# The output projection's second token tile: gates multiplied from SBUF, its operands in attention's buffers

## The chip, the cores and the metric

The kernel runs on one core of a Trainium2 chip. The metric is the device time of one execution in microseconds (us), from the device's own clock.

## What is computed

One transformer block on 1024 tokens of width 1024, all in float32:

```python
h = rmsnorm(x, g_mix_pre)
proj = h @ w_in
qa, ka, va, gate_a, beta_a, alpha_a, qb, kb, vb = split(proj)
out_a = gated_deltanet(...) * silu(gate_a)      # 4 heads x 128
out_b = dilated_attention(qb, kb, vb, rel_bias) # 8 heads x 64
mix = concatenate([out_a, out_b]) @ w_out       # the output projection
x = x + rmsnorm(mix, g_mix_post)
h = rmsnorm(x, g_ffn_pre)
x = x + rmsnorm((silu(h @ w_gate) * (h @ w_up)) @ w_down, g_ffn_post)
```

## The kernel before, in words

**How the program is made.** Every piece of work is a Python generator, a strand, that yields one instruction after another. A scheduler in the kernel file keeps a modelled clock for each engine, takes at each step the strand whose next instruction can start first (with priorities, and on TensorE with a margin of 850 ns for operands that would only just be there), and so fixes each engine's order of instructions when the program is built. On the chip each engine runs its list in that order, and an instruction that waits for a semaphore holds everything behind it on its engine. All large transfers are issued from SyncE (SP, "SPq" in the profile), one list in order.

**The order of the work.** The input projections (tiles `pj`), then the delta-rule chain and the attention beside the last projections, then the output projection, then the gated feed-forward layer (gate and up products and the down product, PSUM tiles `bank`). The feed-forward products are made by a seven-product scheme on 2 x 2 blocks.

**Matrix products in three parts.** Each float32 operand is split into a high part (a cast, `mh`, `woh`, `wbh`) and a low part (a subtraction, `ml`, `wol`, `wbl`); a product takes three matmuls, high x high, high x low, low x high (`mm3`).

**The output projection** (`out_proj`, line 1809) runs over eight token tiles t of 128 tokens. The mixer's 1024 channels come in two parts: part 0 is the delta rule's four heads, part 1 the attention's. A tile has two column halves b of 512, and for each half and part 4 channel blocks x 3 matmuls of 128 x 512 into the PSUM tile `pw`: 48 matmuls a tile. Tile 0 takes them in the order part 0 for both halves, then part 1 for both; the others take part 0 and part 1 of half 0, then of half 1. When a half is done ScalarE copies it out (`evacuate`, tile `y`).

**What feeds it** (`mix_load`, line 1738; `mix_loads` runs it for t = 0 to 7, part 0 then part 1, one strand, each load requested once the one before has issued its split). For each tile and part: load `mx` (256 KB) from the DRAM tensor `d_mix`; for part 1, multiply by `rp`, the softmax denominators spread over PSUM by four small matmuls; for part 0, multiply by the gates; then split into `mh` and `ml`. The gates lie in SBUF tiles `gst`. `gate_silu` (line 837) applies SiLU to them and stores all eight to DRAM (`d_gt`). Tile 0 multiplies straight from the four `gst` tiles that hold tokens 0 to 511 (`first`), one 128 x 128 multiply for each head; then `first_done` releases them. Every later tile waits until all gates are projected (`ev_gates`), and loads its gates back from `d_gt` into a tile `gt` (one 128 x 512 multiply).

**Buffers.** `mx` of tile 0 lies in a small pool `ax`, that of all others in two slots (`mxS`) which are also the last two gates' buffers (`rawS.slots[:2]`, line 1668); so such a load waits until those gates are stored. `mh` and `ml` of the others take slots `mixS`.

**Afterwards** (`residual`, line 1842): for each tile load `x3` (the block's input, two halves), square sum of `y` (`junk`), multiply by `gpost`, `n_m` and `n_r` (an inverse root: DVE, then GpSimd), add (`x`, two halves), second square sum, second `n_r`, scale (`y`), eight transposes on TensorE (two groups of four, `tp`), which ScalarE copies to `h2s` for tiles 0 to 3 and stores as `d_h2`.

**The feed-forward's start.** `ev_ax` fires when tile 0's matmuls are issued (line 1829). The build then closes the pool stack `s2`, which holds attention's pool `at` and `ax` (line 1899), and takes the feed-forward's pools in that memory; only then are its strands made, the weight loads (`wraw`) and splits (`wbh`, `wbl`) among them. The first four `wraw` loads come in that way amid the output projection; the matmuls that use them begin when all eight tiles are through.

Of the kernel before, what the change touches and what calls it, by code (L numbers as in the profile page):

```python
# [11 lines left out]
F32 = mybir.dt.float32  # L12
F32R = mybir.dt.float32r
BF16 = mybir.dt.bfloat16
AF = mybir.ActivationFunctionType
ALU = mybir.AluOpType
# [5 lines left out]
P = 128  # L22
# [24 lines left out]
SB = 4  # L47
XB = 3
# [11 lines left out]
def sub(ap, dims, off=0):  # L60
    return bass.AP(tensor=ap.tensor, offset=ap.offset + off, ap=[list(d) for d in dims])
# [480 lines left out]
def block_kernel(ctx: ExitStack, tc: tile.TileContext, a, out):  # L542
    nc = tc.nc
    w = Weaver(nc)
    T, V, A, G, SY = (Engine(w, e, k) for e, k in (
        (nc.tensor, "PE"), (nc.vector, "V"), (nc.scalar, "A"), (nc.gpsimd, "G"), (nc.sync, "S")))
    ctx.enter_context(tc.manual_schedule(engines={ENG.PE, ENG.DVE, ENG.Activation, ENG.Pool, ENG.SP}))

    def mm(out, lhsT, rhs, start=True, stop=True):
        return T.matmul(out, lhsT, rhs, start=start, stop=stop)  # L550

    def tr(out, in_):
        return T.transpose(out, in_, ident[:])

    def mm3(ps, lh, ll, rh, rl, first, last):
        return [mm(ps, lh, rh, first, False), mm(ps, lh, rl, False, False), mm(ps, ll, rh, False, last)]
# [9 lines left out]
    def split_sb(hi, lo, src):  # L566
        yield Either(A.copy(hi, src), V.tensor_copy(hi, src), bias=BIAS)
        yield Either(*[e.tensor_tensor(lo, src, hi.bitcast(F32), ALU.subtract) for e in (V, G)])

    def pool(stack, name, bufs, space=None, side=None):  # L570
        return Pool(w, stack, tc, name, bufs, space, side)
# [256 lines left out]
    gates, silued, silu, first = [], [], set(), {}  # L828
# [526 lines left out]
    at = pool(s2, "at", 2)  # L1355
# [310 lines left out]
    woS, mixS, mxS, x3S = (Slots(wp, "", 0) for _ in range(4))  # L1666
# [66 lines left out]


    axS = Slots(pool(s2, "ax", 1), "ax", 5)
    mixes = {}
    ev_mix = [[Event() for _ in range(2)] for _ in range(NT)]
    def mix_load(t, part):

        tl = slice(t * P, (t + 1) * P)  # L1740
        if part:
            for m in range(PAIRS):
                yield ev_att[m][t // 2]
        else:
            yield ev_o[t]
        if t:
            yield ev_gates
        x = yield (mxS if t else axS).get([P, 4, P], F32, name="mx")
        yield SY.dma_start(x[:], d_mix[4 * part:4 * part + 4, :, tl].rearrange("k p j -> p k j"))
        if part:  # L1750

            if t % 4 == 0:
                r = psums[:, t:t + 4, :]
                yield V.reciprocal(r, r)
                yield from split_sb(rtok[:, :, 0:AH], rtok[:, :, AH:2 * AH], r)
                tp = yield banks.get([P, P], F32, name="rt")
                yield tr(tp[:], rtok[:].rearrange("p t k -> p (t k)").bitcast(F32))
                for k in range(4):

                    x32 = rrow[32 * k:32 * k + 32, k, :]  # L1760
                    yield A.copy(sub(x32, [list(x32.ap[0]), [-1, 4], [-4, 32]], 127),
                                 tp[32 * k:32 * k + 32, :].rearrange("p (r j) -> p r j", r=4))
                banks.put(tp)
            rp = yield banks.get([P, 4, P], F32, name="rp")
            yield [mm(rp[:, m, :], spread[:, m, :], rrow[:, t % 4, :]) for m in range(4)]
            yield After(x[:])
            yield V.tensor_tensor(x[:], x[:], rp[:], ALU.mult)
            banks.put(rp)
        elif t:
            f = yield gtS.get([P, 4, P], F32, name="gt")  # L1770
            yield ev_gt
            yield SY.dma_start(f[:], d_gt[:, :, tl].rearrange("k p j -> p k j"))
            yield After(x[:], f[:])
            yield Either(*[e.tensor_tensor(x[:], x[:], f[:], ALU.mult) for e in (V, G)])
            gtS.put(f)
        else:

            yield ev_silu
            yield After(x[:])
            for h in range(GH):  # L1780
                yield Either(*[e.tensor_tensor(x[:, h, :], x[:, h, :], first[h][:, 0:P], ALU.mult) for e in (V, G)])
            w.spawn(first_done(), 3)
        hi = yield (mixS if t else axS).get([P, 4, P], F32R, name="mh")
        lo = yield (mixS if t else axS).get([P, 4, P], F32R, name="ml")
        yield from split_sb(hi[:], lo[:], x[:])
        axS.put(x)
        mixes[t, part] = hi, lo
        ev_mix[t][part].fire()

    def first_done():  # L1790
        yield ev_gt
        outS.put(*first.values())

    def mix_loads():
        for t in range(NT):
            for part in (0, 1):
                yield from mix_load(t, part)
# [11 lines left out]
    def out_proj():  # L1809
        for t in range(NT):  # L1810
            evs, ys, ps = [], {1: Event()}, []
            parts = [(0, 0), (1, 0), (0, 1), (1, 1)] if t else [(0, 0), (0, 1), (1, 0), (1, 1)]
            for part, b in parts:
                if not part:
                    z = yield banks.get([P, 512], F32, name="pw")
                    ps.append(z)
                yield ev_mix[t][part]
                mh, ml = mixes[t, part]
                for k in range(4):
                    yield ev_wo[4 * part + k][b]  # L1820
                    yield mm3(ps[b][:], mh[:, k, :], ml[:, k, :], *(z[:, k, :] for z in wo[part, b]),
                              part == 0 and k == 0, part == 1 and k == 3)
                if t == NT - 1:
                    hS.put(*wo[part, b])
                if part:
                    evs.append(w.spawn(evacuate(ys, b, ps[b]), 0))
            axS.put(*mixes[t, 0], *mixes[t, 1])
            if t == 0:
                ev_ax.fire()
            w.spawn(residual(t, ys, evs), 0 if t == NT - 1 else 2)  # L1830

# [2 lines left out]
    def evacuate(ys, b, ps):  # L1834
        if b == 0:
            ys[0] = yield pr.get([P, D], F32, name="y3")
            ys[1].fire()
        yield ys[1]
        yield A.copy(ys[0][:, b * 512:b * 512 + 512], ps[:])
        banks.put(ps)  # L1840

    def residual(t, ys, evs):
# [49 lines left out]
        ev_tr[t].fire()  # L1892

    done_proj = w.spawn(out_proj(), 9)
    w.run(ev_main, ev_gates, *[e for x in ev_q2 + ev_k2 + ev_v for e in x])
    sh.close()
# [555 lines left out]
```

## Time and profile before

| | us |
|---|---|
| three runs | 1224.42, 1224.97, 1222.09 (median 1224.42) |
| the profiled execution, its own time | 1225.21 |
| its span, first to last instruction | 1223.4 |
| TensorE busy in it | 1203.1 (98%) |
| VectorE (DVE) busy | 884.5 |
| ScalarE (ACT) busy | 546.3 |
| GpSimd (POOL) busy | 157.3 |
| mean granted TensorE clock | 0.996 |

In a timeline row stand the start, the time from the first start to the last end of the row's instructions, engine, line, operation, tiles, shapes, the count, and in brackets how long the engine had been idle and what released it. Nearly all instructions carry line 286, where a helper records them; so they are told apart by their tiles. In a row of waits stand the engine, its tile, who was waited for, the total in us, how often, and the longest. Durations of neighbours on an engine overlap by some tenths, so positions are read from starts. In a row of windows stand the stretch, its length, busy time and count for TensorE, the granted clock, the DMA engines' busy share and GB/s.

### The profile page before, as it was taken

What the parts mean: (1) busy time and instruction counts of PE and PEld (TensorE: products, weight loads), DVE (VectorE), ACT (ScalarE), POOL (GpSimd) and SP (SyncE); (2) the same over time, 40 slices, a digit from 0 to 9 for tenths busy, and PEclk for the clock granted to TensorE, in tenths of its full rate; (3) what the DMA queues carried; (4) which work ended last, traced back from release to release, by engine and by line L of the source; (5) the groups of instructions that cost most, each with busy time, mean ns of one, the idle gap of its engine ahead of it and who ended that gap; (6) DMA issues with size and microseconds to landing.
All of it is one profiled execution on the core that took longest, in us unless ns stands there. A gap on an engine that the chain in (4) does not pass through costs nothing.

```text
span 1223.4 us, 19593 instructions
## 1 busy us (share of the span) xinstructions
PE 1203.1 (98%) x7135; PEld 998.1 (82%) x7135; DVE 884.5 (72%) x1627; ACT 546.3 (45%) x1063; POOL 157.3 (13%) x138
## 2 busy tenths in 40 slices
PE   8999999999999999899999999999999999999997
PEld 6878798788888778788788888888888888888886
DVE  4689969646665756666998876877668767876886
ACT  6655521226665654454643323333333334544541
POOL 0143411001111100001100110111001100000111
PEclk9999999999999999899999999999999999999999
DMA  7655363667546355674544433322343239645335
GB/s 266 207 148 168 104 181 105 135 230 243 188 148 208 106 169 170 217 231 146 183 154 139 138 112 130 120 82 83 104 129 121 74 108 321 229 138 147 103 121 206
DMA packets 152887, 193.03 MB, mean 158 GB/s; under 512 B 29992, under 2 KB 78376, under 8 KB 152792
## 3 DMA queue, kind: packets, MB, share of 16 engines
q1 hardware_dynamic: 148568, 189.69, 48.2%
q10 hardware_dynamic: 4224, 2.10, 0.6%
q8 instruction: 56, 0.92, 0.3%
q14 instruction: 39, 0.32, 0.1%
HBM read 135.88 MB, written 59.66 MB: 160 GB/s over the span
## 4 chain that ended last, share of the span: by engine, by line
PE 83%; DMA 5%; DVE 5%; ACT 2%; issue 2%; SPq 1%; POOL 1%; DVEq 0%; POOLq 0%; ACTq 0%
PE bank L286 47%; PE pj L286 21%; PE tp L286 4%; PE p L286 3%; PE pw L286 3%; PE pS L286 2%; PE pV L286 2%; PE pm L286 2%; DVE yc L286 1%; DMA xn<-in_x 1%; SPq L286 1%; DMA h2l<-d_h 1%; DVE x L286 1%; ACT junk L286 1%; DMA views<-in_w_down 0%
## 5 line engine op out<-in xcount | busy, mean ns | idle before, releaser
L286 PE MATMUL pj<-hTh,w 128*128 128x512 f32 x768 | 264.1, 405 | 5.8 <-ACT hTh L286 5.8
L286 PEld LDWEIGHTS pj<-hTh,w 128*128 128x128 f32 x768 | 145.5, 189 | 40.5 <-ACT hTh L286 5.8
L286 ACT CAST wbh<-wraw 128x512 fp32r<-128x512 f32 x130 | 80.3, 621 | 199.0 <-PE bank L286 123.8
L286 PE MATMUL pj<-hTl,w 128*128 128x512 f32 x384 | 151.2, 394 | 0.0
L286 DVE TENSOR_TENSOR wbl<-wraw,wbh 128x512 fp32r<-128x512 f32 x131 | 92.2, 706 | 29.2 <-ACT wbh L286 29.0
L286 PE MATMUL bank<-views 128*128 128x512 f32 (+1 forms) x307 | 84.8, 384 | 0.0
L286 PEld LDWEIGHTS pj<-hTl,w 128*128 128x128 f32 x384 | 73.0, 190 | 12.6 <-DVE hTl L286 0.7
L286 PE MATMUL bank<-views,dah 128*128 128x512 f32 (+1 forms) x214 | 73.5, 379 | 0.0
L286 PE MATMUL bank<-dbh,views 128*128 128x512 f32 (+1 forms) x201 | 70.3, 380 | 0.0
L286 PEld LDWEIGHTS bank<-views 128*128 128x128 f32 x307 | 57.5, 188 | 11.4
L286 POOL TENSOR_TENSOR m<-m,m 128x512 f32<-128x512 f32 x18 | 28.3, 1573 | 253.2 <-DVE r L286 179.6
L286 PE MATMUL pw<-woh,mh 128*128 128x512 f32 x128 | 52.9, 413 | 3.5 <-ACT mh L286 3.4
L286 ACT CAST w<-wr 128x512 fp32r<-128x512 f32 x53 | 32.5, 617 | 52.2 <-PE pj L286 46.8
L286 PE MATMUL pw<-woh,ml 128*128 128x512 f32 x128 | 51.0, 398 | 0.0
L286 PE MATMUL pw<-wol,mh 128*128 128x512 f32 x128 | 50.9, 398 | 0.0
L286 PE MATMUL bank<-dbh,dah 128*128 128x512 f32 (+1 forms) x129 | 49.1, 381 | 0.0
L286 DVE TENSOR_TENSOR w<-wr,w 128x512 fp32r<-128x512 f32 x44 | 30.6, 702 | 24.9 <-ACT w L286 23.3
L286 DVE SCALAR_TENSOR_TENSOR yc<-raw,convw,yc 128x1024 f32<-128x1024 f32 x36 | 46.5, 1292 | 0.5
L286 PEld LDWEIGHTS bank<-views,dah 128*128 128x128 f32 x214 | 40.0, 188 | 7.7
L286 PEld LDWEIGHTS bank<-dbh,views 128*128 128x128 f32 x201 | 37.7, 188 | 7.1
L286 DVE TENSOR_TENSOR m<-bank,m 128x512 f32<-128x512 f32 x44 | 30.1, 685 | 18.1 <-PE bank L286 18.0
L286 ACT ACTIVATE Sr<-Sr,mx 128x384 f32<-128x384 f32 (+3 forms) x64 | 38.1, 597 | 6.3 <-DVE mx L286 5.9
(377 smaller groups left out, 3058.1 us busy)
## 6 DMA issues: line engine op xcount, KB each, us to landing
wr<-in_w_in SPq DMA_DIRECT2D x56, 256.0 KB
wraw<-in_w_gate SPq DMA_DIRECT2D x52, 256.0 KB
wraw<-in_w_up SPq DMA_DIRECT2D x52, 256.0 KB
views<-d_hid SPq DMA_DIRECT2D x47, 256.0 KB
db<-in_w_down SPq DMA_DIRECT2D x40, 256.0 KB
da<-d_hid SPq DMA_DIRECT2D x30, 256.0 KB
d_hid<-x SPq DMA_DIRECT2D x22, 256.0 KB
d_hid<-r SPq DMA_DIRECT2D x22, 256.0 KB
```

Source lines behind the costliest of these rows:

```text
L286: op.fn(*op.args, **op.kw)
```

## The change

It concerns tile 1 of the output projection, the second.

```diff
-    mixes = {}
+    mixes, second = {}, []
...
-        if t:
+        if t > 1:
             yield ev_gates
-        x = yield (mxS if t else axS).get([P, 4, P], F32, name="mx")
+        if t == 1:
+            x = yield at.get([P, 4, P], F32, name="mx", tag="Sr", bufs=SB)
+        else:
+            x = yield (mxS if t else axS).get([P, 4, P], F32, name="mx")
...
-        elif t:
+        elif t > 1:
             f = yield gtS.get([P, 4, P], F32, name="gt")
...
-                yield Either(*[e.tensor_tensor(x[:, h, :], x[:, h, :], first[h][:, 0:P], ALU.mult) for e in (V, G)])
-            w.spawn(first_done(), 3)
-        hi = yield (mixS if t else axS).get([P, 4, P], F32R, name="mh")
-        lo = yield (mixS if t else axS).get([P, 4, P], F32R, name="ml")
+                yield Either(*[e.tensor_tensor(x[:, h, :], x[:, h, :], first[h][:, tl], ALU.mult) for e in (V, G)])
+            if t:
+                w.spawn(first_done(), 3)
+        if t == 1:
+            if not part:
+                second.append((yield at.get([P, 4, 4, P], F32R, name="mX", tag="X", bufs=XB)))
+            hi, lo = second[0][:, 2 * part], second[0][:, 2 * part + 1]
+        else:
+            hi = yield (mixS if t else axS).get([P, 4, P], F32R, name="mh")
+            lo = yield (mixS if t else axS).get([P, 4, P], F32R, name="ml")
...
-            if t == 0:
+            if t == 1:
                 ev_ax.fire()
```

Tile 1's gates come from the `gst` tiles that tile 0 uses, by four 128 x 128 multiplies; they are released after tile 1. Its two `mx` tiles lie in attention's score buffers (tag `Sr`, four of them), and its high and low parts in one of attention's `X` buffers, as the tile `mX`. As that memory is in `s2`, `ev_ax` now fires after tile 1. The load `gt` of tile 1 is gone; all else is computed as before. The scheduler then lays the instructions around it anew. From tile 7's residual on the lists of VectorE, ScalarE and GpSimd read as before but for the numbers in names and, at the very end of the program, the order of some short finishing steps.

SP's list behind the last store of gates. Before: `mx_5551` and `mx_5631` are tile 1's parts 0 and 1, `gt_5573` its gates, `x3` the input rows for tile 0's residual, `wraw` the first feed-forward weights.

```order
L286 DMA mx_5551<-d_mix_74 128x4x128
L286 DMA gt_5573<-d_gt_73 128x4x128
L286 DMA x3_5593<-in_x 128x512
L286 DMA x3_5615<-in_x 128x512
L286 DMA wraw_5609<-in_w_gate 128x512
L286 DMA wraw_5618<-in_w_up 128x512
L286 DMA wraw_5625<-in_w_gate 128x512
L286 DMA wraw_5629<-in_w_up 128x512
L286 DMA mx_5631<-d_mix_74 128x4x128
```

Changed: `mx_5551` and `mx_5602` are tile 1's parts, `mx_5624` with `gt_5626` and `mx_5656` are tile 2's.

```order
L286 DMA mx_5551<-d_mix_74 128x4x128
L286 DMA x3_5597<-in_x 128x512
L286 DMA x3_5599<-in_x 128x512
L286 DMA mx_5602<-d_mix_74 128x4x128
L286 DMA mx_5624<-d_mix_74 128x4x128
L286 DMA gt_5626<-d_gt_73 128x4x128
L286 DMA mx_5656<-d_mix_74 128x4x128
```

Tile 1's part 1 stands ahead of the weights, and so do tile 2's loads; `gt_5573` is gone. The weights follow some rows later, behind the input rows of tile 1's residual (`x3_5716`, `x3_5738`) and ahead of tile 3's part 1 (`mx_5759`):

```order
L286 DMA x3_5716<-in_x 128x512
L286 DMA x3_5738<-in_x 128x512
L286 DMA wraw_5732<-in_w_gate 128x512
L286 DMA wraw_5748<-in_w_up 128x512
L286 DMA wraw_5753<-in_w_gate 128x512
L286 DMA wraw_5761<-in_w_up 128x512
L286 DMA mx_5759<-d_mix_74 128x4x128
```

In the program the first of them, `wraw_5732`, waits for a TensorE semaphore, the readers of the memory it goes to; before, `wraw_5609` waited for none.

VectorE's list where the weight splits stand. Before, amid tile 0's residual (`y_5578`; `x_5593` and `x_5615` are its halves), with tile 1's part 1 (`mx<-mx,rp` and the `ml` behind it) in the same stretch:

```order
L286 TENSOR_TENSOR y_5578<-y_5578,gpost 128x1024
L286 TENSOR_SCALAR n_m<-ss_5620 128x1
L286 TENSOR_TENSOR wbl<-wraw,wbh 128x512
L286 SCALAR_TENSOR_TENSOR x_5593<-y_5578,n_r,x_5593 128x512
L286 TENSOR_TENSOR wbl<-wraw,wbh 128x512
L286 SCALAR_TENSOR_TENSOR x_5615<-y_5578,n_r,x_5615 128x512
L286 TENSOR_TENSOR mx<-mx,rp 128x512
L286 TENSOR_TENSOR ss_5620<-ss_5620 128x1
L286 TENSOR_SCALAR n_m<-ss_5620 128x1
L286 TENSOR_TENSOR ml<-mx,mh 128x512
L286 SCALAR_TENSOR_TENSOR y_5578<-x_5593,n_r,gpre 128x512
```

Changed, amid tile 1's residual (`y_5654`), with tile 3's part 1:

```order
L286 TENSOR_SCALAR n_m<-ss_5750 128x1
L286 TENSOR_TENSOR wbl<-wraw,wbh 128x512
L286 SCALAR_TENSOR_TENSOR x_5716<-y_5654,n_r,x_5716 128x512
L286 TENSOR_TENSOR wbl<-wraw,wbh 128x512
L286 SCALAR_TENSOR_TENSOR x_5738<-y_5654,n_r,x_5738 128x512
L286 TENSOR_TENSOR mx<-mx,rp 128x512
L286 TENSOR_TENSOR ss_5750<-ss_5750 128x1
L286 CAST mh<-mx 128x512
L286 TENSOR_SCALAR n_m<-ss_5750 128x1
L286 TENSOR_TENSOR ml<-mx,mh 128x512
L286 SCALAR_TENSOR_TENSOR y_5654<-x_5716,n_r,gpre 128x512
```

The two splits of weights moved from tile 0's residual to tile 1's, and one cast `mh` joined the stretch from ScalarE. On TensorE, tile 0's transposes stand behind the 45th matmul of tile 1 and the 12th of tile 2 (before: behind the 21st and 27th of tile 1); tile 1's stand behind the 42nd and 48th of tile 2 (before: at the 48th, and the 6th of tile 3). The `rp` matmuls of tile 1 stand right ahead of its first matmul (before: behind its 3rd), those of tile 2 behind tile 1's 24th, and those of tile 3 behind tile 2's 12th.

## The prediction

> **What bounds the kernel now.** I read the page's first part, then TensorE's waits, then its timeline and the windows around the longest wait that isn't at the start, then the lists of the engines that this wait leads back to.
>
> ```profile
> span 1223.4 us, 19593 instructions
> PE 1203.1 (98%) x7135; PEld 998.1 (82%) x7135; DVE 884.5 (72%) x1627; ACT 546.3 (45%) x1063; POOL 157.3 (13%) x138
> PE pj L286 <- ACT hTh L286: 5.8, 1, 5.8
> PE pw L286 <- ACT mh L286: 3.4, 1, 3.4
> PE tp L286 <- DVE y L286: 1.2, 2, 0.9
> ```
>
> TensorE (PE) is busy 98% of the span. Only what it waits for, and the rate at which it runs, can change. Of its waits the 3.4 us for `mh`, in the output projection, is the one that the change touches. TensorE's timeline around it:
>
> ```profile
> 480.72 0.40 PE L286 MATMUL pw<-woh,mh 128*128 128x512 f32 x1
> ...
> 490.03 0.39 PE L286 MATMUL pw<-woh,ml 128*128 128x512 f32 x1
> 490.49 0.50 PE L286 MATMUL pw<-woh,mh 128*128 128x512 f32 x1
> ...
> 493.83 0.39 PE L286 MATMUL pw<-woh,ml 128*128 128x512 f32 x1
> 497.61 0.79 PE L286 MATMUL pw<-woh,mh 128*128 128x512 f32 x1 [3.39 <-ACT mh L286]
> ...
> 498.63 0.63 PE L286 MATMUL pw<-woh,ml 128*128 128x512 f32 x1
> 499.05 0.63 PE L286 MATMUL pw<-woh,mh 128*128 128x512 f32 x1
> ...
> 503.73 0.40 PE L286 MATMUL pw<-woh,mh 128*128 128x512 f32 x1
> ...
> 504.20 0.40 PE L286 MATMUL pw<-woh,ml 128*128 128x512 f32 x1
> 504.43 0.60 PE L286 MATMUL tp<-ident,y 128*128 128x128 f32 x4
> ...
> 505.10 0.39 PE L286 MATMUL pw<-wol,mh 128*128 128x512 f32 x1
> ```
>
> At full rate 41 matmuls take 490.03 - 480.72 = 9.31 us, 0.227 us each. A group of four small ones (`tp`; I take the same for `rp`) costs 505.10 - 504.20 - 2 x 0.227 = 0.45. Tile 0 ends at 490.03 + 0.227 = 490.26. Tile 1 begins 0.23 late; at 493.83 its part 0 of half 0 is done and part 1 isn't there. After the wait the matmuls come every 0.42 us until 503.73. The windows say why, and what comes later:
>
> ```profile
> 498.00:504.00 6.00, 6.00 (x18) 0.52 0.53 159
> 504.00:508.00 4.00, 4.00 (x23) 1.00 0.75 247
> 600.00:1200.00 600.00, 599.77 (x2659) 496.36 (x2658) 467.63 (x719) 237.77 (x426) 60.65 (x43) 1.00 0.41 134
> ```
>
> The granted clock is 0.52 in this stretch, 1.00 behind it. From 600 to 1200 TensorE lacks 0.23 us in all: what is won before arrives at the end.
>
> The losses that belong to the wait: 493.83 to 497.61 less one matmul is 3.55. Between 497.61 and 503.73 lie 12 matmuls and one `tp`, 12 x 0.227 + 0.45 = 3.17 of work in 6.12: 2.95 lost to the clock. With tile 1's late beginning that is 3.55 + 2.95 + 0.23 = **6.7 us**.
>
> The Trainium skill's TensorE: Matmul & The Clock Gate, Part 1, has the same pair: one idle window of about 3.4 us halves the clock, and the windows run freely, so whether a gap of that length does it depends on its phase. By that rule the 2.95 could be missing in some executions before; the sum goes by this trace, which has it.
>
> **What the change does, part by part.** First why tile 1 was late. SP's list and one of its waits:
>
> ```profile
> 480.54 1.02 SPq L286 DMA_DIRECT2D d_gt<-gst  x2
> 485.56 0.37 SPq L286 DMA_DIRECT2D mx<-d_mix  x1
> 485.98 0.50 SPq L286 DMA_DIRECT2D gt<-d_gt  x1
> 486.57 0.93 SPq L286 DMA_DIRECT2D x<-in_x  x2
> 487.55 0.42 SPq L286 DMA_DIRECT2D wraw<-in_w_gate  x1
> ...
> 489.44 0.71 SPq L286 DMA_DIRECT2D mx<-d_mix  x1
> SPq L286 <- DMA d_gt<-gst: 3.9, 1, 3.9
> ```
>
> Part 0's `mx` waits 3.9 us for the store of the gates in its slot, and part 1's goes out at 489.44 behind four weight loads. VectorE and ScalarE:
>
> ```profile
> 471.31 0.29 DVE L286 TENSOR_TENSOR mx<-mx,gst 128x128 f32<-128x128 f32 x1
> 483.53 1.28 DVE L286 TENSOR_TENSOR wol<-wor,woh 128x512 fp32r<-128x512 f32 x2
> 489.28 0.69 DVE L286 TENSOR_TENSOR mx<-mx,gt 128x512 f32<-128x512 f32 x1 [4.47 <-DMA gt<-d_gt]
> 494.29 0.74 DVE L286 SCALAR_TENSOR_TENSOR x<-y,n_r,x 128x512 f32<-128x512 f32 x1
> 496.22 0.67 DVE L286 TENSOR_TENSOR mx<-mx,rp 128x512 f32<-128x512 f32 x1
> 498.20 1.41 DVE L286 SCALAR_TENSOR_TENSOR y<-x,n_r,gpre 128x512 f32<-128x512 f32 x2
> 487.80 0.59 ACT L286 COPY y<-pw 128x512 f32<-128x512 f32 x1 [5.49 <-PE pw L286]
> 490.46 0.59 ACT L286 COPY y<-pw 128x512 f32<-128x512 f32 x1 [2.08 <-PE pw L286]
> 493.00 1.15 ACT L286 CAST wbh<-wraw 128x512 fp32r<-128x512 f32 x2 [0.77 <-DMA wraw<-in_w_gate]
> 496.95 0.60 ACT L286 CAST mh<-mx 128x512 fp32r<-128x512 f32 x1
> ```
>
> *How long a load takes.* The weights issued at 487.55 were there at 493.00: 5.45 us. A short one, tile 2's part 1:
>
> ```profile
> 503.75 0.38 SPq L286 DMA_DIRECT2D mx<-d_mix  x1
> 506.89 0.69 DVE L286 TENSOR_TENSOR mx<-mx,rp 128x512 f32<-128x512 f32 x1 [1.13 <-DMA mx<-d_mix]
> ```
>
> 506.89 - 503.75 = 3.14. These are my bounds, 3.1 to 5.45, for each load below.
>
> *Part 0, moved ahead.* Its `mx` no longer waits and goes out at 480.54 + 1.02 = 481.6; it lands by 487.0 at the latest. The multiplies are four of 0.29 in place of one of 0.69: +0.5 us of VectorE, in the 4.47 us in which it idled; uncovered it would cost that 0.5. They end by 488.2. The cast stands on ScalarE behind the copy of 487.80, so from about 488.4; with the low part (0.69) all is there by about 489.8, before 490.26. The 0.23 goes. The load `gt` (0.5 us of SP) and its wait go with it.
>
> *Part 1, moved ahead.* It stands behind the two `x` loads, and they wait for slots that VectorE last reads by 483.53 + 1.28 = 484.8. Two issues of 0.47 later, at 485.8, `mx` goes out and lands by 491.2. Multiply 0.67, cast (now on VectorE; I take 0.5), low part 0.69: the high part is there by 492.4. TensorE needs it after tile 1's `rp` (490.26 + 0.45 = 490.71) and 12 matmuls, at 493.4. The 3.55 goes, and with it the 2.95.
>
> *Tile 2's loads* go out ahead of the weights, some 15 us before TensorE needs them: nothing. *Gates kept longer:* `gst` is released after tile 1's multiply, by 488.2 as above; the next users of its slots, `h2s` and tile 2's operands, come after 494: nothing.
>
> *The weights, moved back: the new wait.* The first of them now waits for TensorE to be through with tile 1, since it goes to memory that `mX` used. When is that? From 490.71, 45 matmuls, one `rp`, one `tp` and 3 matmuls: 490.71 + 48 x 0.227 + 2 x 0.45 = 502.5. Queued behind it on SP are tile 3's part 1 (needed at about 518; it has 14 us) and tile 0's `d_h2` stores (read back for the feed-forward, after 580). Behind the split on ScalarE (`wbh`) and on VectorE (`wbl`) stands tile 1's residual, and TensorE waits for its result with tile 1's transposes. So that chain decides:
>
> - The weights land at 502.6 plus 3.1 to 5.45: 505.7 to 508.05. I take 4.9, nearer to the row of the same load, since fewer loads are queued ahead: 507.5.
> - From the weights to the end of the first `y` half took, in tile 0's residual, 498.20 + 0.70 - 493.00 = 5.9. The rows are the same now but for one cast more on VectorE: 6.4, with 0.1 of signalling 6.5. So 514.0, between 512.2 and 514.55.
> - TensorE is there after 12 matmuls of tile 2, `rp`, `tp` and 30 more: 502.5 + 42 x 0.227 + 0.9 = 512.9.
>
> The wait is 514.0 - 512.9 = **1.1 us**, between 0 and 1.65; I enter 1.3, with 0.2 for tile 0's transposes: they are due at 490.71 + 45 x 0.227 + 0.45 = 501.4, and their `y` was ready at 498.20 + 1.41 = 499.6, a margin that a late load could use up. It is a short gap; the 0.9 in the waits' third row halved nothing.
>
> The Trainium skill's DMA: Bandwidth & Descriptors, Anatomy of one DMA, gives a fixed cost of about 2 us plus the transfer, for the path through GpSimd. By it, as an estimate, the weights would be there by about 505 and there would be no new wait, the first rival's case; the measured 5.45 says that here, with others queued, it is more.
>
> *Sum.* 6.7 - 1.3 = 5.4. The span goes from 1223.4 to 1218.0. The profiled execution took 1225.21, 1.8 more than its span and 0.8 more than the median; so against the median, 1224.42 - 5.4 = **1219.0**.
>
> **The rivals.**
>
> *No new wait.* The weights land within 3.1 us, as the short row has it; then `y` is there at 512.2, before 512.9. Gain 6.7: 1217.7. Against it stands the 5.45 of the very same load.
>
> *The wait comes back with its clock.* The weights come later than 5.45 (x loads and stores queued), the gap at tile 1's transposes grows past about 2.7 us, and the clock halves again. 3.4 + 3.0 lost of 6.7: 1224.1, no change.
>
> *It doesn't do what it says.* Part 1's `mx` is still late, because the `x` loads ahead of it wait for their slots longer than 484.8, and tile 1 stops as before. For it: SP is one list. Against: VectorE's row. 1224.4.
>
> *Slower.* SP is held by the weights' wait for TensorE, and again by the loads of the next weights, whose slots come free only as `wbl` runs; behind them on the list stands tile 4's `mx`. It is needed at about 527 and would go out, as I estimate, at about 512 (behind the stores of tile 1's halves, which come two steps ahead of the 514.0): 10 us of room with its landing. It decides if SP is held over 10 us more; then TensorE stops twice, at the transposes and at tile 4, each with its half clock: 2 x 6.4 - 6.7 = 6.1 lost, 1230.5. Nothing in the trace holds SP that long in this stretch.
>
> **How the numbers follow.** A measurement of this kernel tells about 0.3%, 3.7 us, from no change (the three runs spread over 2.9). Forecast 0.54, no new wait 0.17, the wait with its clock 0.15, not what it says 0.07, slower 0.07. The forecast's own range is 6.7 less 0 to 1.65, with the runs' spread 1217.5 to 1220.5. The first two cases are faster by over 3.7: 0.71, less 0.03 for a wait of over 2 us: 0.68; slower 0.07; the rest 0.25. The range that leaves out 2 in 10 reaches from 1216.5 (the best case with the spread) into the third case: 1223.2.
>
> **What would show it.** Right: in the changed profile tile 1 (`mX`) runs without a gap at full clock from about 490.3; its `mx` goes out at about 481.6 and 485.8; the first amid `wraw` goes out at about 502.5; TensorE waits about 1 us for `y` at tile 1's transposes, near 513; `bank` starts 5.4 us earlier than before. Wrong: a wait for `mX`; a stretch of half clock between 490 and 585; a gap of over 2.7 us near 513; or gaps in 585 to 640 that weren't there, which would mean that the feed-forward's start was held by something else.

## The result, and the profile after

The changed kernel takes **1215.93 us** (median of six executions, 1215.55 to 1217.46), the kernel before 1223.26 (six beside it, 1221.72 to 1224.97): a ratio of 0.9943, 95% interval 0.993 to 0.9956. The forecast was 1219.0, range 1216.5 to 1223.2: the right direction, but the gain of 7.3 us is larger than the 5.4 forecast, and the time lies 0.6 below the range. A second job later gave 1217.85 beside 1223.50; the eleven executions together have a median of 1217.08 (1214.9 to 1219.3). So 7.3 us are gained in the one job and 5.7 in the other. The changed kernel's two medians lie 1.9 apart, three times the 0.6 by which the first misses the range; the second lies inside it.

The profiled execution took 1217.08. Its page and TensorE's waits (engine, tile, who was waited for, total, times, longest):

```profile
span 1215.3 us, 19597 instructions
PE 1198.3 (99%) x7135; PEld 996.0 (82%) x7135; DVE 886.0 (73%) x1633; ACT 544.8 (45%) x1060; POOL 158.0 (13%) x138
```

```profile
PE pj L286 <- ACT hTh L286: 5.1, 1, 5.1
PE tp L286 <- DVE y L286: 1.6, 2, 1.3
```

The row `pw <- mh` of 3.4 is gone; nothing of the output projection stands in it but the waits for `y`. Three rows of TensorE's timeline cut the span into stages: the first matmul of the output projection, the first of the feed-forward, the last. Before:

```profile
478.90 0.39 PE L286 MATMUL pw<-woh,mh 128*128 128x512 f32 x1
...
584.25 0.40 PE L286 MATMUL bank<-B11h,wbh 128*128 128x512 f32 x1
...
1215.97 0.28 PE L286 MATMUL bank<-dbh,views 128*128 128x256 f32 x1
```

After:

```profile
476.74 0.39 PE L286 MATMUL pw<-woh,mh 128*128 128x512 f32 x1
...
574.88 0.40 PE L286 MATMUL bank<-B11h,wbh 128*128 128x512 f32 x1
...
1207.82 0.28 PE L286 MATMUL bank<-dbh,views 128*128 128x256 f32 x1
```

| stage | before | after | |
|---|---|---|---|
| up to the output projection | 478.90 | 476.74 | -2.16 |
| output projection | 105.35 | 98.14 | -7.21 |
| feed-forward | 631.72 | 632.94 | +1.22 |
| tail, to the end of the span | 7.43 | 7.48 | +0.05 |

The first 2.16 lie ahead of anything that the change touches, and that point lay between 476.2 and 478.9 in the profiles of all kernels below: they are the two executions' own. The change's are the 7.21, less perhaps the 1.22.

In the projection, TensorE's timeline of tile 1 (`mX`):

```profile
487.88 0.39 PE L286 MATMUL pw<-woh,ml 128*128 128x512 f32 x1
488.10 0.56 PE L286 MATMUL rp<-rrow,spread 128*128 128x128 f32 x4
488.50 0.45 PE L286 MATMUL pw<-woh,mX 128*128 128x512 f32 x1
...
500.18 0.40 PE L286 MATMUL pw<-woh,mX 128*128 128x512 f32 x1
...
510.61 0.39 PE L286 MATMUL pw<-woh,ml 128*128 128x512 f32 x1
511.34 0.44 PE L286 MATMUL tp<-ident,y 128*128 128x128 f32 x2 [0.34 <-DVE y L286]
```

From 488.50 to 500.18 lie 47 matmuls, one `rp` and one `tp`: 47 x 0.227 + 2 x 0.45 = 11.57, and 11.68 were taken. Tile 1 has no gap. At its transposes TensorE stops: 511.34 - 510.61 - 0.227 = 0.50. The same stretches of windows as before (length, busy time and count of PE, PEld, DVE, ACT, POOL, granted clock, DMA share, GB/s):

```profile
498.00:504.00 6.00, 6.00 (x35) 5.08 (x33) 3.67 (x7) 2.94 (x5) 0.22 (x1) 1.00 0.81 242
600.00:1200.00 600.00, 599.08 (x2657) 495.94 (x2656) 461.40 (x708) 231.52 (x415) 60.68 (x44) 1.00 0.42 137
```

The clock stays at 1.00. From 600 to 1200 TensorE now lacks 0.92 us where it lacked 0.23: that is part of the 1.22 lost in the feed-forward.

SP's list:

```profile
478.38 1.02 SPq L286 DMA_DIRECT2D d_gt<-gst  x2
479.45 0.49 SPq L286 DMA_DIRECT2D mx<-d_mix  x1
482.09 0.93 SPq L286 DMA_DIRECT2D x<-in_x  x2
483.07 1.14 SPq L286 DMA_DIRECT2D mx<-d_mix  x2
...
500.61 0.33 SPq L286 DMA_DIRECT2D wraw<-in_w_gate  x1
...
502.46 0.38 SPq L286 DMA_DIRECT2D mx<-d_mix  x1
```

Part 0's `mx` no longer waits for the gates' stores, part 1's goes out with tile 2's part 0 at 483.07, the weights at 500.61, and tile 3's part 1 at 502.46 behind them. ScalarE and VectorE, where these loads are used:

```profile
503.18 0.62 ACT L286 CAST wbh<-wraw 128x512 fp32r<-128x512 f32 x1 [0.80 <-DMA wraw<-in_w_gate]
```

```profile
503.83 0.69 DVE L286 TENSOR_TENSOR wbl<-wraw,wbh 128x512 fp32r<-128x512 f32 x1
...
508.21 0.69 DVE L286 TENSOR_TENSOR mx<-mx,rp 128x512 f32<-128x512 f32 x1 [1.49 <-DMA mx<-d_mix]
...
510.53 1.41 DVE L286 SCALAR_TENSOR_TENSOR y<-x,n_r,gpre 128x512 f32<-128x512 f32 x2 [0.45 <-POOL n_r L286]
```

The weights are there 503.18 - 500.61 = 2.57 us after their issue. VectorE is then held 1.49 us by tile 3's part 1, which took 508.21 - 502.46 = 5.75 and stands in its list in front of tile 1's residual.

### The profile page after: what moved, and what is told of

It is laid out like the page before. It is cut to its first block, busy times and chain, and to the rows that moved or that the text cites. A ratio compares the mean times of both kernels' runs of the same rounds, so it can differ in the third digit from the quotient of the medians.

```text
span 1215.3 us, 19597 instructions
## 1 busy us (share of the span) xinstructions
PE 1198.3 (99%) x7135; PEld 996.0 (82%) x7135; DVE 886.0 (73%) x1633; ACT 544.8 (45%) x1060; POOL 158.0 (13%) x138
## 4 chain that ended last, share of the span: by engine, by line
PE 90%; DVE 4%; DMA 2%; issue 1%; ACT 1%; POOL 1%; SPq 0%; DVEq 0%; POOLq 0%; ACTq 0%
PE bank L286 48%; PE pj L286 22%; PE pw L286 6%; PE tp L286 5%; PE p L286 3%; PE pS L286 2%; PE pV L286 2%; PE pm L286 2%; DVE yc L286 1%; DMA views<-in_w_down 1%; DMA mx<-d_mix 0%; SPq L286 0%; DMA db<-in_w_down 0%; DMA cbv<-d_bv 0%; DVE x L286 0%
## 5 line engine op out<-in xcount | busy, mean ns | idle before, releaser
L286 PE MATMUL pw<-woh,mh 128*128 128x512 f32 x112 | 45.2, 404 | 0.0
L286 PE MATMUL pw<-woh,ml 128*128 128x512 f32 x112 | 43.8, 391 | 0.0
L286 PE MATMUL pw<-wol,mh 128*128 128x512 f32 x112 | 43.7, 390 | 0.0
```

Of the source, the lines that this page charges most:

```text
L286: op.fn(*op.args, **op.kw)
```

## The experiments

Twelve runs, each timed beside the kernel before. "Projection" and "feed-forward" are the stages of the table above, in the run's own profile.

**The kernel before, again.**

> The kernel before, unchanged, timed against itself: the six runs so far lie near 1222.1 (three) and near 1224.5 (three). Theory (the half clock behind the wait for tile 1 comes in some executions and not in others): the mean granted clock is about 0.996 in runs near 1224.5 and about 0.999 in runs near 1222.1, a difference of some 2.4 to 3.0 us. Rival (the start differs, when the first loads land and when the clock first rises): the recorded clock is the same in both groups, and the place of the first output-projection matmul differs by 1 to 2.5 us between profiles. Ratio 1.000 within 0.002.

1223.81 (1221.06 to 1224.65, eleven executions), ratio 1.0005 [0.9996, 1.0014]. Its profile has the wait and not the half clock; TensorE's timeline and the window behind it:

```profile
497.35 0.50 PE L286 MATMUL pw<-woh,mh 128*128 128x512 f32 x1 [3.32 <-ACT mh L286]
```

```profile
494.00:500.00 6.00, 2.68 (x12) 1.86 (x12) 4.96 (x10) 1.95 (x5) 0.56 (x1) 1.00 0.70 209
```

The projection took 102.13 here, 3.2 less than the 105.35 of the execution with the half clock. Two of the eleven executions have a mean clock of 0.999 and took 1221.06 and 1222.06; the nine others have 0.996 or 0.997 and a median of 1223.85. By these two the half clock costs 2.3 us where it comes. Of all 61 executions of the kernel before whose clock is on record, in three jobs, 24 have 0.996 and a median of 1223.95, 26 have 0.997 and 1222.86, seven have 0.998 or 0.999 and 1222.05 (four have 0.995, and 1223.8). So it comes in most executions, not in all to the same extent, and costs some 1 to 2 us of the time. A mean clock doesn't say where in the execution it was low; only the two profiles do.

**One part at a time.** The change has three: tile 1's gates from SBUF, the weights let go a tile later, the buffers. Gates only:

```diff
-        elif t:
+        elif t > 1:
             f = yield gtS.get([P, 4, P], F32, name="gt")
...
-                ... first[h][:, 0:P], ALU.mult) for e in (V, G)])
-            w.spawn(first_done(), 3)
+                ... first[h][:, tl], ALU.mult) for e in (V, G)])
+            if t:
+                w.spawn(first_done(), 3)
```

> One part alone: tile 1's gates come from SBUF, its load of gates is gone; its mixer loads and operands stay in the old slots, and the feed-forward's strands still start after tile 0. Theory (part 1's load behind the four weight loads is what stops TensorE): the wait of 3.4 us before tile 1's second group stays, 2.5 to 3.5 us, and the time changes by 0 to -1 us. Rival (the gates' way through DRAM is what made tile 1 late): the wait goes, -6 to -7 us.

1227.52, ratio 1.0031 [1.0019, 1.0043]: slower. Its waits:

```profile
PE pw L286 <- ACT mh L286: 4.3, 1, 4.3
PE bank L286 <- DVE wbl L286: 2.7, 1, 2.7
```

Tile 1 still stops; taking the gates from SBUF does nothing for part 1, which is behind the weights as before. And a wait is new in the feed-forward (631.72 before, 636.27 here), to which the last experiments return.

Weights only, from before:

```diff
-            if t == 0:
+            if t == 1:
                 ev_ax.fire()
```

> One part alone: the feed-forward's strands start after tile 1 in place of tile 0; gates and buffers as before. Theory (weights ahead of part 1's load): part 1's load goes out ahead of the weights, the wait of 3.4 us goes with the half clock behind it, -5 to -7.5 us; a short wait at the start of tile 1 stays or grows (its first mixer load still waits for the gates' store, and its gates come from DRAM), 0.2 to 1 us. Rival (it needs the buffers or the gates as well): the wait for tile 1 stays at 2 us or more, time -2 us or less.

1219.51, ratio 0.997 [0.9959, 0.9982]: 3.6 us less than the 1223.13 beside it, short of the 5 expected. The projection takes 100.16, and no execution has a clock under 0.998. Tile 1 still stops twice, and no half clock follows:

```profile
494.50 0.50 PE L286 MATMUL pw<-woh,mh 128*128 128x512 f32 x1 [1.16 <-ACT mh L286]
495.94 0.50 PE L286 MATMUL pw<-woh,ml 128*128 128x512 f32 x1 [0.71 <-DVE ml L286]
```

This one line, alone, gives the larger part of the gain.

Weights and buffers without the gates (the changed kernel, with tile 1's gates loaded back):

```diff
-        elif t > 1:
+        elif t:
...
-            if t:
-                w.spawn(first_done(), 3)
+            w.spawn(first_done(), 3)
```

> All but the gates: tile 1's mixer loads and operands lie in attention's buffers, the feed-forward's strands start after tile 1, but the gates of tile 1 still come from DRAM. Theory: as the changed kernel within 1 us, -6 to -7.5 us, since the gates' load is some 4 us ahead of need once the mixer load no longer waits. Rival (gates): tile 1 starts 1 to 4 us late, waiting for the gates' load, and the time is between the two kernels, 0 to -4 us.

1221.63 (ten executions; an eleventh took 4219.23, for no reason that is known, and is left out), ratio 0.9983 [0.9974, 0.9992]. Its projection takes 98.74, nearly the changed kernel's 98.14: without buffers that wait for the gates' stores tile 1 doesn't stop, though its gates are loaded back. But its feed-forward takes 635.02, with 2.7 us of waiting for `wbl`. So its time, read without its stages, would credit the gates with what the feed-forward lost.

Gates and weights without the buffers (the two diffs above, from before):

> Gates from SBUF and the feed-forward's strands after tile 1, but all buffers as before: tile 1's first mixer load still waits for the store of the gates in its slot. Theory (weights' place is most of it, buffers give the rest): the output projection takes 98.5 to 100 us (98.1 in the changed kernel, 100.2 with the weights' place alone), with 0.5 to 1.5 us of late beginning of tile 1; the total, which also hangs on the order the scheduler finds for the feed-forward's start, 1217 to 1222. Rival (buffers matter little): no wait in tile 1, as the changed kernel within 0.5 us.

1229.38, ratio 1.0048 [1.0033, 1.0063], projection 108.0. Tile 1 is in time, and tiles 3 and 4 stop instead, each at its part 1:

```profile
518.99 0.58 PE L286 MATMUL pw<-woh,mh 128*128 128x512 f32 x1 [1.97 <-DVE mh L286]
535.89 0.50 PE L286 MATMUL pw<-woh,mh 128*128 128x512 f32 x1 [2.18 <-ACT mh L286]
```

```profile
519.50:522.50 3.00, 3.00 (x11) 2.32 (x10) 2.27 (x5) 0.66 (x2) 0.55 (x1) 0.50 0.81 241
```

VectorE's rows ahead of these stops:

```profile
506.14 0.69 DVE L286 TENSOR_TENSOR wbl<-wraw,wbh 128x512 fp32r<-128x512 f32 x1 [5.07 <-ACT wbh L286]
...
517.31 0.68 DVE L286 TENSOR_TENSOR mx<-mx,rp 128x512 f32<-128x512 f32 x1
...
533.37 1.23 DVE L286 TENSOR_TENSOR y<-y,gpost 128x1024 f32<-128x1024 f32 x1 [3.14 <-ACT junk L286]
534.51 0.68 DVE L286 TENSOR_TENSOR mx<-mx,rp 128x512 f32<-128x512 f32 x1
```

Neither multiply waits for its load. Tile 3's stands in VectorE's list behind two weight splits, for which VectorE stood 5.07 us, and behind tile 1's whole residual; in the weights-only kernel it stands ahead of that residual's adds. Tile 4's stands behind the first step of a residual, for which VectorE waited 3.14. So by the trace it is the order made by the scheduler that brings these stops; that the old buffers have a direct part in them isn't shown. The wait of 1.97 us was followed by a half clock.

**The wait without its idling.** From before, 14 matmuls whose result nobody reads fill most of tile 1's wait:

```diff
+                if t == 1 and (part, b) == (1, 0):
+                    spare = yield banks.get([P, 512], F32, name="spare")
+                    for n in range(14):
+                        yield mm(spare[:], mh[:, 0, :], wo[0, 0][0][:, 0, :], n == 0, n == 13)
+                    banks.put(spare)
```

> The kernel before with 14 extra matmuls into a spare PSUM tile, which nothing reads, right where TensorE waits for tile 1's part 1: the wait is there as before, but TensorE is busy in it. This prices the half clock by itself. Theory (of the 6.7 us, 3 are the clock, in the executions that have it): the granted clock stays 1.00 from 480 to 585, the first output-projection matmul to the first feed-forward one takes 101.5 to 102.5 us (105.4 with and 102.1 without the half clock in the two profiles of before), and the median falls by 1.5 to 2.8 us. Rival (the clock's loss is given back later, or the extra work costs as much): within 0.7 us of before.

1222.57, ratio 0.9993 [0.9984, 1.0001]; the clock is 0.998 or 0.999 in all twelve executions. The other engines' lists are those of the kernel before.

```profile
492.22 3.33 PE L286 MATMUL spare<-woh,mh 128*128 128x512 f32 x14
496.23 0.50 PE L286 MATMUL pw<-woh,mh 128*128 128x512 f32 x1 [0.67 <-ACT mh L286]
```

The stop is a little longer (496.23 - 492.22 = 4.01 against 3.55) and the half clock is gone. With the 0.46 that the longer stop takes back, the clock alone is worth 0.7 + 0.46 = 1.2 us by these medians (1223.24 beside it), and up to 2.4 by the interval's end; the 2.3 above lies within. The median fell by 0.7, where 1.5 to 2.8 was expected; the rival's "within 0.7" fits it as well. In the stage more is seen: the projection takes 102.96, 2.4 less than the 105.35 with the half clock, and 2.9 with the 0.46. Why the times show less isn't settled; that not every execution of the kernel before has the whole half clock is part of it. The larger rest of the gain is the wait itself.

**The new wait.** The changed kernel with the weights let go after tile 2 instead of tile 1, twice:

```diff
-            if t == 1:
+            if t == 2:
                 ev_ax.fire()
```

> The changed kernel with the feed-forward's strands one tile later still, after tile 2. Theory (the 0.5 us wait at tile 1's transposes comes of the weights' loads, which hold up tile 3's part 1 on SP and so tile 1's residual on VectorE): that wait goes, the output projection takes 97.4 to 97.8 us in place of 98.1; total -0.3 to -0.8 us against the changed kernel unless the feed-forward's start is laid otherwise. Rival (the weights are then late for the feed-forward): a wait of bank at its first groups, +1 us or more.

1217.35, ratio 0.9953 [0.9941, 0.9965], projection 97.67. VectorE no longer waits for tile 3's part 1, and TensorE doesn't stop at tile 1's transposes; the last matmul ahead of them and they stand 0.23 apart in the second run:

> The changed kernel with the weights' loads let go after tile 2 instead of tile 1, once more and beside the changed kernel. If the 0.5 us that TensorE waits at tile 1's transposes are the whole of what the later weights save, it comes out 0.3 to 0.6 under the run of the changed kernel beside it (1215.4 to 1215.7); if something later takes them back, equal to it within 0.3.

```profile
509.42 0.39 PE L286 MATMUL pw<-woh,ml 128*128 128x512 f32 x1
509.65 0.60 PE L286 MATMUL tp<-ident,y 128*128 128x128 f32 x4
```

1216.60, ratio 0.995 [0.9936, 0.9963]; the changed kernel in the same job:

> The changed kernel once more, beside the other three. Both theories: 1216.0 (1215.4 to 1217.5), no half clock in any execution, projection phase 97.5 to 98.2, feed-forward 632 to 633.2. If the feed-forward's 1.2 us over the kernel before in the first profile belong to the change, they stand here again; if they are scatter between executions, the feed-forward is 631 to 632.

1217.85, ratio 0.9955 [0.9943, 0.9968], projection 98.09, feed-forward 633.21. The 0.4 seems to be there in the stage (97.67 twice, against 98.14 and 98.09). But the last kernel of this section has the changed kernel's lists through the whole projection, and it took 97.70, with hardly a stop at tile 1's transposes:

```profile
512.14 0.39 PE L286 MATMUL pw<-woh,ml 128*128 128x512 f32 x1
512.41 0.66 PE L286 MATMUL tp<-ident,y 128*128 128x128 f32 x4
```

So the same lists stop TensorE there for 0.50, 0.31 and 0.04 us in three executions, and VectorE for 1.49, 1.32 and 1.04. What the later weights show is VectorE's wait gone in both profiles; what they are worth to TensorE is within the scatter. In the second job they came out 1.25 lower, twice what was expected. In the times of both jobs the two can't be told apart: ten executions of the one have a median of 1217.3, eleven of the other 1217.08. So no version tried is shown to beat the changed kernel.

**Gates of four tiles from SBUF.** From the changed kernel, tiles 2 and 3 too take their gates from `first`:

```diff
-        elif t > 1:
+        elif t > 3:
...
-            if t:
+            if t == 3:
                 w.spawn(first_done(), 3)
```

> The changed kernel with tiles 2 and 3 too taking their gates from SBUF (the four gst tiles hold tokens 0 to 511), two more loads of gates gone. Theory (gates were never what TensorE waited for): the output projection as in the changed kernel within 0.5 us, total within 1 us of it unless the feed-forward's start is laid otherwise. Rival (each load less on SP helps): -1 us or more in the output projection.

1219.47, ratio 0.9972 [0.9961, 0.9983]: projection 97.95, as in the changed kernel, but the feed-forward 635.26, with the wait for `wbl` again (2.1 us).

**What the feed-forward lost.** The changed kernel's lists in the feed-forward are those of before, row for row. The four kernels with the wait for `wbl` have another order there, though nothing in the feed-forward was edited: the scheduler made it from other times in its model. VectorE's rows, after:

```profile
599.69 0.68 DVE L286 TENSOR_TENSOR wbl<-wraw,wbh 128x512 fp32r<-128x512 f32 x1
600.29 0.68 DVE L286 TENSOR_TENSOR T1l<-h2l,T1h 128x512 fp32r<-128x512 f32 x1
600.89 1.78 DVE L286 TENSOR_TENSOR T3l<-h2r,T3h 128x512 fp32r<-128x512 f32 x1
602.60 1.27 DVE L286 TENSOR_TENSOR x<-bank,m 128x512 f32<-128x512 f32 x2
```

In the buffers-only kernel:

```profile
601.52 1.78 DVE L286 TENSOR_TENSOR T1l<-h2l,T1h 128x512 fp32r<-128x512 f32 x1
603.23 1.27 DVE L286 TENSOR_TENSOR x<-bank,m 128x512 f32<-128x512 f32 x2
604.43 0.67 DVE L286 TENSOR_TENSOR T4l<-h2l,T4h 128x512 fp32r<-128x512 f32 x1
605.03 1.28 DVE L286 TENSOR_TENSOR wbl<-wraw,wbh 128x512 fp32r<-128x512 f32 x2
```

A `wbl` comes behind the two `x<-bank` instead of ahead of them. Two kernels test that. In the buffers-only kernel one subtraction is given to GpSimd, (t, n) = (0, 2), by which that `wbl` comes ahead again:

```diff
-        for dst, x, y in ((b11, b12, b11), ...):
-            yield Either(*[e.tensor_tensor(dst[:], x[:], y[:], ALU.subtract) for e in (V, G)])
+        for n, (dst, x, y) in enumerate(((b11, b12, b11), ...)):
+            yield Either(*[... for e in ((G,) if (t, n) == (0, 2) else (V, G))])
```

> The buffers-only kernel with one subtraction ahead of the feed-forward given to GpSimd, by which one low part wbl comes ahead of the two x out of banks on VectorE, as in the kernel before. Theory (buffers_only lost to the changed kernel by the order of the feed-forward's start, 2.7 us of wait and a half clock in some executions, and hardly in the projection): no wait for wbl near 603, feed-forward 631 to 633, projection 98 to 99, time 1216.3 to 1218. Rival (the gates from SBUF carry that gain themselves): the time stays over 1220.5.

1218.72 in place of 1221.63, ratio 0.9964 [0.9951, 0.9976]; no wait for `wbl`, feed-forward 632.56. Its projection, 99.85, is 1.1 longer than it was, though every list up to the feed-forward reads the same: TensorE waited for `y` at four tiles' transposes in this execution (1.4 us in all, tile 7's with them). So stages of single profiles scatter by 1 us. The time is above the range expected. And in the changed kernel the same edit with (3, 2), which leaves every list up to the feed-forward as it was:

> The changed kernel with one subtraction of the feed-forward given to GpSimd, which leaves every list up to there as it was and puts one low part wbl behind the two x out of banks on VectorE. Theory: TensorE waits 2 to 3 us for that wbl near 602, in some executions with a half clock behind it, feed-forward 634.5 to 637, projection as in the changed kernel, time 1218 to 1221. Rival (the wait there is hidden or made good behind): within 0.5 of the changed kernel.

1218.66, ratio 0.9968 [0.9956, 0.9981]; projection 97.7, feed-forward 634.99. TensorE:

```profile
605.49 0.50 PE L286 MATMUL bank<-B11h,wbl 128*128 128x512 f32 x1 [2.02 <-DVE wbl L286]
```

With that row behind the two `x<-bank` the wait is there, ahead of them it is gone: 1.8 to 2.1 us of the stage here (634.99 against 633.21 and 632.94). The edits move other rows behind 597 us as well, so that it is this row alone is read from TensorE's wait, not tested. In the medians it is 0.8 against the run beside it, with intervals that overlap.

## Why the prediction was wrong in size

**Right: the bound and the mechanism.** Tile 1's wait, the half clock behind it and the late beginning went, all three. Measured from the projection's first matmul, part 0's `mx` went out at 2.7 (forecast 481.6 - 478.90 = 2.7), part 1's at 6.3 (485.8: 6.9), the first of the weights at 23.9 (502.6: 23.7); the wait that takes the old one's place came where it was put, at tile 1's transposes. The experiments show that moving the weights behind part 1 gives most of it by itself. The rest of tile 1's stop went with the buffers added (buffers only), and also with the gates added (gates and weights); so neither is shown to be the one that is needed. With both other parts in place the gates have no share that could be measured: without them the projection is 0.6 longer, by a single profile, which is within the scatter.

**The step that failed: the new wait, 1.3 us, and in it "The weights land ... I take 4.9".** They landed in 2.57, and in 2.59 and 2.62 in two more profiles of these lists. The 5.45 of the kernel before was that load with other loads under way; in its new place it met fewer. The windows of the two loads, before and after (the last two numbers are the DMA engines' share and GB/s):

```profile
487.55:493.00 5.45, 5.38 (x25) 3.92 (x24) 2.55 (x4) 2.33 (x4) 0.00 (x0) 1.00 0.90 287
500.61:503.18 2.57, 2.57 (x13) 2.08 (x12) 1.28 (x2) 1.74 (x4) 0.00 (x0) 1.00 0.64 214
```

I knew of that and took off 0.55; the short row, 3.14, was the nearer one. The price that the Trainium skill's DMA: Bandwidth & Descriptors, Anatomy of one DMA, leads to (about 2 us and the transfer, as an estimate 2.6, stated there for the path through GpSimd) agrees with the 2.57 here and not with the 5.75 of tile 3's part 1, queued behind the weights.

**A second step was wrong the other way.** From the weights to the end of the first `y` half I took 6.5. It was 510.53 + 0.70 - 503.18 = 8.05, and 1.49 of that is VectorE waiting for tile 3's part 1. I had named that load as queued behind the weights, and dismissed it since TensorE needs it only 14 us later. VectorE doesn't need it either, but stands still for it: in an ordered list what counts is who is *behind* the consumer. That VectorE's wait makes TensorE's is argued from the trace; that VectorE's goes with the weights' place is shown by the later weights. Of the two errors, 2.3 too late and 1.6 too early, most cancels, which is luck: TensorE waited 0.50 us, and 0.31 and 0.04 in the other two profiles, where 1.1 was worked out and 1.3 entered; at tile 0's transposes, for which 0.2 of it stood, it didn't stop. In the first profile that is 0.8 of the gap.

**What the execution added.** In the profile of before, TensorE also lost small times at the transposes of tiles 4 and 5 for want of `y`. The second one:

```profile
570.11 0.39 PE L286 MATMUL pw<-woh,ml 128*128 128x512 f32 x1
570.78 0.41 PE L286 MATMUL tp<-ident,y 128*128 128x128 f32 x2 [0.28 <-DVE y L286]
```

570.78 - 570.11 - 0.227 is 0.44, and at tile 4's some 0.2 was lost. In the changed kernel they aren't there; but neither are they in the second profile of the kernel before, so they are that execution's and no gain of the change. With them 6.7 + 0.6 - 0.50 = 6.8 of the 7.21 are found. The other 0.4 I can't name.

**The base, and the clock's price.** I subtracted from 1224.42, the median of three. Six give 1223.26, and later jobs 1223.13 to 1223.50. That is 1.2 of the 3.1 between forecast and result. The second job's gain, 1223.50 - 1217.85 = 5.65, is close to the 5.4. The Trainium skill's TensorE: Matmul & The Clock Gate, Part 1, had said that the half clock depends on how the idle time falls, and the kernel before shows it: a profile with it, a profile without. A profile of one execution, priced as if it were the median, has that error in it: the term of 2.95 for the half clock stands in the stage of that profile, but in the times the half clock was worth 1 to 2.4 us. So the parts found don't add up to the gain in the times, and that remains open. The Trainium skill's one idle window of about 3.4 us, in that section, isn't the least gap either: 1.97 us were followed by a half clock in the kernel with gates and weights, and the measurement decides. The prediction put the half clock's return past 2.7 us; 2.66 were followed by it in the gates-only kernel, and by none in the buffers-only kernel.

**The rivals.** The nearest was that no new wait comes (1217.7), and its reason, weights that land within 3.1, held; it missed the chain behind them, which left up to 0.50. The wait did not come back with its clock, and SP was not held. A gap in 585 to 640 that grew, one of the signs of being wrong, did come: tile 7's, below. What I had not priced is that the order of the feed-forward can change without an edit; in the two kernels that test it, it costs 1.8 to 2.5 us, as much as a whole term of my sum. The changed kernel kept the old order; of the variants, four did not.

**Open:** most of the 1.22 of the feed-forward. It came again in the second profile of the changed kernel (633.21); the kernel before, with the same lists there, has 631.72, 631.13 and, with the extra matmuls, 631.84. So some of it goes with the change. Tile 7's wait for `y` is such a part: 1.26, 1.22 and 1.26 us in three profiles of the changed lists, 0.91, 0.78 and 0.76 in those of before. The waits where the down products begin (0.24 for `views` and 0.68 for `dal` in the changed kernel's profile, 0.23 for `dal` before) are less sure: the kernel with later weights has 0.67 for `dal` in one profile and none in the other.

## What to carry to other kernels

Price a move by two questions: what is late next and what stands in a list behind the instruction that waits for it; an operand that is needed much later can still hold the engine that prepares it. Compare variants by stages, since a scheduler that orders the whole program can take back in a stage that nobody edited what an edit won. And before subtracting from a median, ask how many of its executions have the loss that the one profile shows.

## What the runs showed of the hardware

- The clock after an idle TensorE is not a matter of the idle time alone. 3.39 us brought a clock of 0.52 in one execution of the kernel before, 3.32 left it at 1.00 in another; 2.66 us were followed by 0.50 in the gates-only kernel, and by 1.00 in the buffers-only kernel. 1.97 us were followed by a half clock in the kernel with gates and weights.
- A 256 KB load took 2.57 to 5.75 us from its issue to its first use. The weights' load took 2.57 with the DMA engines' share at 0.64 in that stretch and 5.45 with 0.90; loads of `mx` took 3.14 with 0.65 and 5.75 with 0.94. That the share is the cause is argued from these four.
